# Rows for accumulating DMAs loaded one quarter ahead, their negative right behind the copy of the quarter's opening piece

## The chip, the core and the metric

The kernel runs on one core of one Trainium2 chip. The metric is the device time of one execution in microseconds; the time of the kernel before is the median of three runs. Five engines work beside each other, each in the order of its own instructions: TensorE (PE, with its weight loads as PEld), VectorE (DVE), ScalarE (ACT), GpSimd (POOL) and SyncE (SP). They wait for one another by semaphores. SP, POOL and ACT also issue DMAs.

## The reference

Two layers over 256 tokens of width 2048: each is a norm, a token mixer, a residual add, a norm, a SwiGLU feed-forward block (FFN) and a residual add. Layer 0 has an mLSTM as its mixer, layer 1 an RG-LRU. The change touches only the FFN:

```python
def swiglu(x, w_in, w_out):
    g, u = jnp.split(x @ w_in, 2, axis=-1)
    return (jax.nn.silu(g) * u) @ w_out

...
        h = h + mix
        h = h + swiglu(rms_norm(h, norm_ffn[layer]), ffn_w_in[layer], ffn_w_out[layer])
```

`w_in` is 2048 x 11264 and `w_out` 5632 x 2048, in float32.

## The kernel before

Every float32 product is made of three matmuls. A weight is split into a rounded high part and the low part that is left, an activation likewise, and `product` (L830 to L833) adds high x high (L831), high x low of the weight (L832) and low x high (L833). `split` (L267) makes the two parts of a weight: ACT casts (`L268`), DVE subtracts (`L269`).

The FFN (`ffn`, L810) goes through the 5632 inner columns in eleven **steps** `j` of 512. In a step, `inner` (L835) multiplies the normed input with 512 columns of the gate half and 512 of the up half of `w_in`, in eight pairs `p` of row blocks. Most pairs use seven products of sums of blocks in place of eight; the pairs' weights are `raw`, split into `whix`, `wlox` (of the blocks themselves) and `whit`, `wlot` (of their sums), and the first pair, which is done plainly, into `whi`, `wlo`. At the end of a step PSUM banks `P...` and `Q...` are drained by ACT and DVE into `ds` (L867 to L890), which becomes the step's output `v`; `turn_v` transposes it into `hh`.

The down projection of a step, `hh` with 512 rows of `w_out`, is not done in its own step. `outs` (L906) makes eight **pieces** of it: four quarters `q` of 512 output columns by two blocks `b` of tokens. `between` (L982) runs one piece per pair `p` of the following steps, in the middle of the pair's products. A quarter's opening piece is b = 0, and it loads the quarter. A piece (L951) copies the residual `h` into a PSUM bank (L965, ACT), adds twelve matmuls to it, and copies it back (L976, ACT; these copies are kept in the list `copies`).

The weights of a quarter are four row blocks. Rows 0 and 1 come by SP into `rawo` and are split by ACT and DVE (`whio`, `wloo`). Rows 2 and 3 take work off DVE. POOL loads them into a buffer (named `rawo` in even quarters, `whio` in odd ones, L939), ACT writes the negative of it to `wloo` rounded (L944), POOL issues a second DMA of the same rows that adds them to that negative (L945, the **accumulating DMA**), so that `wloo` holds the low part, and ACT rounds the buffer in place to the high part (L946). The negative is kept behind the copy of the piece before the last one by `after`, which fixes an order between two instructions; otherwise a scheduler orders each engine, and `tc.high_priority(offset=AHEAD)` lets it take an instruction earlier than the place at which it is written.

```python
                            with after(*copies[-2:-1]):
                                nc.scalar.activation(wl, raw, AF.Copy, scale=-1.0)
                            nc.gpsimd.dma_start(wl, src, accum_op=ALU.add)
                            nc.scalar.copy(wh, raw)
```

After step 10 the pieces that are left of step 9 and the eight of step 10 are done in one go, with loads and splits of four row blocks at once (the branch `last` in `load`). In the first step the load of rows 2 and 3 is held back until `v` is there, by a copy of one element on POOL (L938), since the buffers' space is used by something else before.

## Time and profile before

| | |
|---|---|
| median of three runs | 2182.32 us (2180.9 to 2183.56) |
| profiled execution | 2184.34 us |
| its span, first to last instruction | 2182.4 us |
| mean granted TensorE clock | 0.976 |
| DMA | 446.66 MB, mean 205 GB/s |

The span falls into the mLSTM mixer up to about 404 us, the first FFN up to about 1145, the RG-LRU mixer up to about 1440, and the second FFN with the final norm. Times in rows are microseconds from the start of the span. A row of the timeline has start, duration, engine, line, operation, output and inputs; in brackets stands the engine's idle time just before and what ended it. A row of the list of waits has the total, the number and the longest wait. A row that ends in `DMA to landing` has the shortest, median and longest time from the issue of a DMA to its landing. Buffer numbers are left out of the names in the profile: `wloo` is each of the low parts of the down projection.

### The profile page before, as it was taken

How to read it: one execution, taken by the hardware profiler on the slowest of the kernel's cores; microseconds unless marked ns; L12 is line 12 of the kernel's file. 1: busy time of each engine (PE TensorE's matmuls, PEld its weight loads, DVE VectorE, ACT ScalarE, POOL GpSimd, SP SyncE). 2: the span in 40 equal slices, each digit the busy share in tenths (PEclk: the TensorE clock that was granted, in tenths of full speed). 3: DMA queues.
4: the chain of work that ended last, by engine and by line, in shares of the span. 5: the costliest groups of instructions: out<-in, count | busy, mean ns of one | idle time of the engine just before them, and what ended most of it. 6: DMA issues, size and time to landing. Idle time of an engine off the chain costs nothing.

```text
span 2182.4 us, 27890 instructions
## 1 busy us (share of the span) xinstructions
PE 2088.9 (96%) x10430; PEld 1761.3 (81%) x10430; DVE 1736.0 (80%) x1920; ACT 1435.8 (66%) x1755; POOL 205.8 (9%) x222
## 2 busy tenths in 40 slices
PE   9999999998899898989999999999889999898998
PEld 8988888877788787878879999887778778787886
DVE  6655556688799797998976797768879979798896
ACT  5345445556677676867865777655668767686775
POOL 0011110011111110111100000001111111111112
PEclk9999999999999999999999999999999999999999
DMA  7556566566787786886855666656668768688684
GB/s 227 170 163 179 175 194 211 174 204 182 200 256 218 196 247 195 234 243 197 239 175 166 193 189 207 212 174 203 190 202 252 223 193 250 194 236 246 192 237 150
DMA packets 233119, 446.66 MB, mean 205 GB/s; under 512 B 16328, under 2 KB 17048, under 8 KB 232856
## 3 DMA queue, kind: packets, MB, share of 16 engines
q1 hardware_dynamic: 189832, 362.02, 50.1%
q0 software_dynamic: 42432, 81.80, 18.6%
q8 instruction: 81, 1.33, 0.2%
q10 hardware_dynamic: 720, 1.07, 0.1%
q14 instruction: 54, 0.44, 0.1%
HBM read 442.74 MB, written 2.10 MB: 204 GB/s over the span
## 4 chain that ended last, share of the span: by engine, by line
PE 82%; DMA 6%; issue 6%; DVE 2%; ACT 2%; POOL 1%; POOLq 0%; ACTq 0%; SPq 0%; DVEq 0%
PE out L832 7%; PE out L833 7%; PE out L831 6%; PE P L832 6%; PE P L833 6%; PE P L831 5%; DMA wloo<-in_ffn_w_out_dram 5%; PE Q L831 5%; PE Q L832 5%; PE Q L833 5%; PE po L328 3%; PE po L330 3%; PE po L329 3%; PE v L328 1%; PE o L330 1%
## 5 line engine op out<-in xcount | busy, mean ns | idle before, releaser
L244 DVE TENSOR_TENSOR wlo<-raw,whi 128x1024 fp32r<-128x1024 f32 (+1 forms) x226 | 273.6, 1213 | 173.8 <-ACT whi L243 171.4
L268 ACT CAST whit<-sum 128x1024 fp32r<-128x1024 f32 x284 | 296.3, 1052 | 153.9 <-DVE sum L312 147.8
L269 DVE TENSOR_TENSOR wlot<-sum,whit 128x1024 fp32r<-128x1024 f32 x284 | 346.5, 1222 | 54.6 <-ACT whit L268 52.9
L243 ACT CAST whi<-raw 128x1024 fp32r<-128x1024 f32 (+1 forms) x226 | 234.2, 1042 | 194.7 <-PE po L330 40.2
L832 PE MATMUL out<-wloo,hh 128*128 128x512 f32 x704 | 281.6, 400 | 69.1 <-DMA wloo<-in_ffn_w_out_dram 69.0
L269 DVE TENSOR_TENSOR wlox<-raw,whix 128x1536 fp32r<-128x1536 f32 x142 | 249.0, 1754 | 5.1 <-ACT whix L268 4.8
L268 ACT CAST whix<-raw 128x1536 fp32r<-128x1536 f32 x142 | 210.7, 1484 | 37.6 <-PE P L833 32.8
L832 PEld LDWEIGHTS out<-wloo,hh 128*128 128x128 f32 x704 | 134.5, 191 | 102.9 <-DMA wloo<-in_ffn_w_out_dram 73.3
L831 PE MATMUL out<-whio,hh 128*128 128x512 f32 x544 | 212.6, 391 | 1.5 <-ACT whio L268 1.2
L833 PE MATMUL out<-whio,hh 128*128 128x512 f32 x544 | 211.5, 390 | 0.7 <-DVE hh L546 0.7
L976 ACT COPY h<-out 128x512 f32<-128x512 f32 x154 | 89.9, 584 | 169.7 <-PE out L833 169.1
L312 DVE TENSOR_TENSOR sum<-raw 128x1024 f32<-128x1024 f32 x142 | 173.8, 1224 | 3.6
L945 POOL DMA_DIRECT2D wloo<-in_ffn_w_out_dram x78 | 93.3, 1197 | 723.3 <-ACT wloo L944 691.5
L269 DVE TENSOR_TENSOR wloo<-rawo,whio 128x1024 fp32r<-128x1024 f32 (+1 forms) x88 | 118.1, 1342 | 8.6 <-ACT whio L268 8.4
L831 PEld LDWEIGHTS out<-whio,hh 128*128 128x128 f32 x544 | 102.1, 188 | 25.4 <-ACT out L965 2.4
L831 PE MATMUL Q<-whit,p_f 128*128 128x512 f32 x284 | 111.5, 393 | 9.7 <-ACT whit L268 9.7
L833 PEld LDWEIGHTS out<-whio,hh 128*128 128x128 f32 x544 | 102.1, 188 | 22.1 <-DVE hh L546 1.1
L832 PE MATMUL P<-wlox,p_f 128*128 128x512 f32 x284 | 114.6, 403 | 0.0
L268 ACT CAST whio<-rawo 128x1024 fp32r<-128x1024 f32 (+1 forms) x88 | 101.2, 1150 | 18.9 <-PE out L833 16.8
L833 PE MATMUL P<-whix,p_f 128*128 128x512 f32 x284 | 113.2, 398 | 0.0
L831 PE MATMUL P<-whit,p_f 128*128 128x512 f32 x284 | 111.2, 392 | 0.0
L831 PE MATMUL P<-whix,p_f 128*128 128x512 f32 x284 | 111.0, 393 | 0.0
(307 smaller groups left out, 5470.6 us busy)
## 6 DMA issues: line engine op xcount, KB each, us to landing
raw<-in_ffn_w_in_dram SPq DMA_DIRECT2D x352, 512.0 KB, 5.3
rawo<-in_ffn_w_out_dram SPq DMA_DIRECT2D x98, 512.0 KB, 6.2
raw<-in_m_w_in_dram SPq DMA_DIRECT2D x94, 512.0 KB, 3.8
wloo<-in_ffn_w_out_dram POOLq DMA_DIRECT2D x78, 512.0 KB, 7.5
raw<-in_r_w_in_dram SPq DMA_DIRECT2D x64, 512.0 KB, 3.9
rawo<-in_ffn_w_out_dram POOLq DMA_DIRECT2D x40, 512.0 KB, 4.8
whio<-in_ffn_w_out_dram POOLq DMA_DIRECT2D x38, 512.0 KB, 5.3
raw<-in_m_w_out_dram SPq DMA_DIRECT2D x32, 512.0 KB, 3.7
```

The lines of the kernel that those rows point to most:

```text
L243: nc.scalar.copy(hi[:, i:i + step, 0:ncols], r)
L244: nc.vector.tensor_tensor(lo[:, i:i + step, 0:ncols], r, hi[:, i:i + step, 0:ncols].bitcast(F32), op=ALU.subtract)
L268: nc.scalar.copy(hi, src)
L269: nc.vector.tensor_tensor(lo, src, hi.bitcast(F32), op=ALU.subtract)
L312: nc.vector.tensor_tensor(t[:, 0:2, :], raw[:, 1:3, :], raw[:, 3:4, :].broadcast_to([P, 2, NB]), op=ALU.add)
L328: nc.tensor.matmul(o, lhsT=ah[:, bs], rhs=hi, start=(k == 0), stop=False)
L330: nc.tensor.matmul(o, lhsT=al[:, bs], rhs=hi, start=False, stop=(k == nk - 1))
L831: nc.tensor.matmul(o, lhsT=a[0], rhs=b[0], start=start, stop=False, **kw)
L832: nc.tensor.matmul(o, lhsT=a[0], rhs=b[1], start=False, stop=False, **kw)
L833: nc.tensor.matmul(o, lhsT=a[1], rhs=b[0], start=False, stop=stop, **kw)
L945: nc.gpsimd.dma_start(wl, src, accum_op=ALU.add)
L976: copies.append(nc.scalar.copy(hs, o))
```

## The change

Rows 2 and 3 of a quarter are loaded by a function of their own, `load_ahead`, which is run at the second piece (b = 1) of the quarter before; the first of all is run when the first step's pieces are made. The load is ordered behind the last accumulating DMA (`adds`), and the negative behind the newest copy of a piece (`copies[-1:]`, which is that of the opening piece of the running quarter) in place of the one before the newest. The preload of the second piece (`nc.scalar.copy(o, hs)`) is ordered behind the rounding of the buffer. The copy of one element on POOL ahead of the first load from SP is left out. The pieces of a step are made after pair 1 of the next step (after pair 2 in step 1), before it after pair 3; so the quarters' pieces run in pairs 3 to 7 and 0 to 2, and three pieces are left at the end instead of four.

```diff
-        fresh, copies = [True], []
+        fresh, copies, adds, coming = [True], [], [], []
...
-                for i in range(2):
-                    src = wv[:, 2 * i:2 * i + 2, q * NB:(q + 1) * NB]
...
-                    if i == 0:
-                        raw, wh, wl = buffer("raw", F32, ""), buffer("whi", F32R, ""), buffer("wlo", F32R, "")
-                    else:
-
-                        wh, wl = buffer(("raw", "whi")[q % 2], F32R, ""), buffer("wlo", F32R, ("", "1")[q % 2])
-                        raw = wh.bitcast(F32)
+                raw, wh, wl = (buffer(what, dt, 0, q) for what, dt in (("raw", F32), ("whi", F32R), ("wlo", F32R)))
+                nc.sync.dma_start(raw, wv[:, 0:2, q * NB:(q + 1) * NB])
+                with tc.high_priority(offset=AHEAD):
+                    split(wh, wl, raw)
+                for wh, wl in ((wh, wl), ahead.pop(q)):
+                    tiles.extend((wh[:, k, :], wl[:, k, :]) for k in range(2))
...
+            def load_ahead(q):
+
+                wh = buffer(("raw", "whi")[q % 2], F32R, 1, q)
+                wl = buffer("wlo", F32R, 1, q, ("", "1")[q % 2])
+                ahead[q] = wh, wl
+                src = wv[:, 2:4, q * NB:(q + 1) * NB]
+                with tc.high_priority(offset=AHEAD):
                     if j == 0 and q == 0:
 
-                        nc.gpsimd.tensor_copy((wh if i else raw)[0:1, 0, 0:1], v[0][0:1, 0:1])
-                    (nc.gpsimd if i else nc.sync).dma_start(wh if i else raw, src)
-                    with tc.high_priority(offset=AHEAD):
-                        if i:
-
-                            with after(*copies[-2:-1]):
-                                nc.scalar.activation(wl, raw, AF.Copy, scale=-1.0)
-                            nc.gpsimd.dma_start(wl, src, accum_op=ALU.add)
-                            nc.scalar.copy(wh, raw)
-                        else:
-                            split(wh, wl, raw)
-                    tiles.extend((wh[:, k, :], wl[:, k, :]) for k in range(2))
+                        nc.gpsimd.tensor_copy(wh[0:1, 0, 0:1], v[0][0:1, 0:1])
+                    with after(*adds[-1:]):
+                        nc.gpsimd.dma_start(wh, src)
+                    with after(*copies[-1:]):
+                        nc.scalar.activation(wl, wh.bitcast(F32), AF.Copy, scale=-1.0)
+
+                    adds.append(nc.gpsimd.dma_start(wl, src, accum_op=ALU.add))
+                    return nc.scalar.copy(wh, wh.bitcast(F32))
+
+
+            coming.extend(lambda q=q: load_ahead(q) for q in range(4) if j < NJ - 1)
+            if j == 0:
+                coming.pop(0)()
...
                 if not first:
-                    with tc.high_priority(offset=AHEAD):
+
+                    done = [coming.pop(0)()] if b and coming and not last else []
+                    with after(*done), tc.high_priority(offset=AHEAD):
                         nc.scalar.copy(o, hs)
...
-            if left == 0 and p == 3 and late:
+
+            if left == 0 and p == (2 if j == 1 else 1) and late:
```

On POOL the queue of DMAs in two steps in the middle of a layer stood so before (`rawo` and `whio` are the loads, `wloo` the accumulating DMAs):

```order
L939 DMA rawo_4945<-in_ffn_w_out_dram 128x2x512
L939 DMA whio_5081<-in_ffn_w_out_dram 128x2x512
L945 DMA wloo_4946<-in_ffn_w_out_dram 128x2x512
L945 DMA wloo_5082<-in_ffn_w_out_dram 128x2x512
L939 DMA rawo_5199<-in_ffn_w_out_dram 128x2x512
L945 DMA wloo_5200<-in_ffn_w_out_dram 128x2x512
```

And on POOL now, for three quarters in the middle of a layer:

```order
L947 DMA rawo_4838<-in_ffn_w_out_dram 128x2x512
L951 DMA wloo_4839<-in_ffn_w_out_dram 128x2x512
L947 DMA whio_4966<-in_ffn_w_out_dram 128x2x512
L951 DMA wloo_4967<-in_ffn_w_out_dram 128x2x512
L947 DMA rawo_5102<-in_ffn_w_out_dram 128x2x512
L951 DMA wloo_5103<-in_ffn_w_out_dram 128x2x512
```

In every second step the next load stood between a load and its accumulating DMA; now each accumulating DMA stands right behind its own load and ahead of the next.

On ACT, at the end of such a step before (`P_4` is a PSUM bank of the step that ends, `ds` its output, `whi_0` to `whit_1` weights of the next step, `out` the bank of a piece):

```order
L867 COPY ds_5410<-P_4_5504 128x512
L872 COPY ds_5410<-P_4_5504 128x512
L268 CAST whi_0_5914<-raw_0_5911 128x2048
L884 ACTIVATE ds_5410<-ds_5410,rstd_f_3779 128x512
L268 CAST whio_5940<-rawo_5939 128x1024
L944 ACTIVATE wloo_5946<-rawo_5945 128x1024
L976 COPY h<-out_5873 128x512
L946 CAST rawo_5945<-rawo_5945 128x1024
L965 COPY out_5951<-h 128x512
L268 CAST whix_1_5994<-raw_1_5987 128x1536
```

And on ACT now, at the end of the same step:

```order
L867 COPY ds_5436<-P_4_5524 128x512
L872 COPY ds_5436<-P_4_5524 128x512
L268 CAST whi_0_5940<-raw_0_5937 128x2048
L884 ACTIVATE ds_5436<-ds_5436,rstd_f_3779 128x512
L986 COPY h<-out_5899 128x512
L949 ACTIVATE wloo_5967<-whio_5966 128x1024
L268 CAST whix_1_6014<-raw_1_6007 128x1536
L952 CAST whio_5966<-whio_5966 128x1024
L975 COPY out_5965<-h 128x512
```

The negative (L949) has moved behind the copy of the opening piece of quarter 2 (L986), and it is now that of quarter 3; the preload of the second piece (L975) has moved behind the negative, `whix` and the rounding (L952). On TensorE the end of an earlier step reads so now (`out_4965` is the second piece); ahead of these rows stand nine matmuls of pair 7, and ahead of them the opening piece's last:

```order
L831 MATMUL P_3_4944<-whi_0_4940,p_f_3097 128x512
L832 MATMUL P_3_4944<-wlo_0_4941,p_f_3097 128x512
L833 MATMUL P_3_4944<-whi_0_4940,p_f_3097 128x512
L831 MATMUL P_3_4944<-whi_0_4940,p_f_3097 128x512
L832 MATMUL P_3_4944<-wlo_0_4941,p_f_3097 128x512
L833 MATMUL P_3_4944<-whi_0_4940,p_f_3097 128x512
L831 MATMUL P_3_5024<-whix_1_5014,p_f_3118 128x512
L831 MATMUL P_3_4944<-whix_1_5014,p_f_3118 128x512
L831 MATMUL out_4965<-whio_4894,hh_4435 128x512
```

The second piece's first matmul is the eighteenth after the opening piece's last; at the other quarters it is the twenty-fifth.

At the start of a layer's second step ACT had, before:

```order
L545 CAST hh_3995<-tv 128x512 x2
L268 CAST whio_4189<-rawo_4188 128x1024
L944 ACTIVATE wloo_4196<-rawo_4195 128x1024
L946 CAST rawo_4195<-rawo_4195 128x1024
L268 CAST whit_2_4098<-sum_2_4090 128x1024
L268 CAST whi_3_4128<-raw_3_4125 128x2048
L268 CAST whix_4_4163<-raw_4_4156 128x1536
L268 CAST whit_2_4098<-sum_2_4090 128x1024
```

and has now:

```order
L545 CAST hh_3995<-tv 128x512 x2
L949 ACTIVATE wloo_4126<-rawo_4125 128x1024
L952 CAST rawo_4125<-rawo_4125 128x1024
L268 CAST whit_2_4098<-sum_2_4090 128x1024
L268 CAST whi_3_4135<-raw_3_4132 128x2048
L949 ACTIVATE wloo_4217<-whio_4216 128x1024
L268 CAST whit_2_4098<-sum_2_4090 128x1024
L268 CAST whix_4_4190<-raw_4_4183 128x1536
```

A second negative, whose rows POOL loads after the first accumulating DMA, stands ahead of the second half of `whit_2`; before, the load, the negative and the accumulating DMA of that quarter were done ahead of the step.

More of the change, by code (lines that the diff above doesn't have):

```diff
@@ L923, in load @@
                     return
-                for i in range(2):
-                    src = wv[:, 2 * i:2 * i + 2, q * NB:(q + 1) * NB]
-                    def buffer(what, dtype, at):
-                        return pool_of(f"{what}o{at}").tile([P, 2, NB], dtype, tag=f"{what}{i}", name=f"{what}o{j}{q}{i}")
-                    if i == 0:
-                        raw, wh, wl = buffer("raw", F32, ""), buffer("whi", F32R, ""), buffer("wlo", F32R, "")
-                    else:
-                        wh, wl = buffer(("raw", "whi")[q % 2], F32R, ""), buffer("wlo", F32R, ("", "1")[q % 2])
-                        raw = wh.bitcast(F32)
-                    if j == 0 and q == 0:
-                        nc.gpsimd.tensor_copy((wh if i else raw)[0:1, 0, 0:1], v[0][0:1, 0:1])
-                    (nc.gpsimd if i else nc.sync).dma_start(wh if i else raw, src)
-                    with tc.high_priority(offset=AHEAD):
-                        if i:
-                            with after(*copies[-2:-1]):
-                                nc.scalar.activation(wl, raw, AF.Copy, scale=-1.0)
-                            nc.gpsimd.dma_start(wl, src, accum_op=ALU.add)
-                            nc.scalar.copy(wh, raw)
-                        else:
-                            split(wh, wl, raw)
-                    tiles.extend((wh[:, k, :], wl[:, k, :]) for k in range(2))
@@ new lines, in load, with buffer @@
+                raw, wh, wl = (buffer(what, dt, 0, q) for what, dt in (("raw", F32), ("whi", F32R), ("wlo", F32R)))
[4 more added lines that the diff above has]
+                    tiles.extend((wh[:, k, :], wl[:, k, :]) for k in range(2))
+            ahead = {}
+            def buffer(what, dtype, i, q, place=""):
+                return pool_of(f"{what}o{place}").tile([P, 2, NB], dtype, tag=f"{what}{i}", name=f"{what}o{j}{q}{i}")
```

## The prediction

> **What bounds the kernel now.** The page's first part names the engine, the chain of waits says what else stands on the path, and the list of waits says how often.
>
> ```profile
> PE 2088.9 (96%) x10430; PEld 1761.3 (81%) x10430; DVE 1736.0 (80%) x1920; ACT 1435.8 (66%) x1755; POOL 205.8 (9%) x222
> PE 82%; DMA 6%; issue 6%; DVE 2%; ACT 2%; POOL 1%; POOLq 0%; ACTq 0%; SPq 0%; DVEq 0%
> PE out L832 <- DMA wloo<-in_ffn_w_out_dram: 69.0, 10, 7.5
> PE Q L831 <- ACT whit L268: 9.7, 4, 4.6
> ```
>
> TensorE carries the end. It waits for one thing that matters: ten times, 69.0 us together, for the accumulating DMA that makes the low part `wloo` of rows 2 and 3 of a quarter; 9.7 us go to ACT. The chain in order of time has the ten as five in each FFN layer, one for every second step (one pass of the loop over `j`); the second and the last of the first layer:
>
> ```profile
> 571.47 10.65 DMA wloo<-in_ffn_w_out_dram
> ...
> 970.94 10.69 DMA wloo<-in_ffn_w_out_dram
> ```
>
> The timeline around the first shows why it is late.
>
> ```profile
> 570.09 1.08 ACT L944 ACTIVATE wloo<-rawo 128x1024 fp32r<-128x1024 f32 x1
> 570.53 0.72 POOL L939 DMA_DIRECT2D whio<-in_ffn_w_out_dram  x1 [14.46 <-ACT whio L268]
> 571.47 1.22 POOL L945 DMA_DIRECT2D wloo<-in_ffn_w_out_dram  x1 [0.22 <-issue]
> ...
> 582.16 0.80 PE L832 MATMUL out<-wloo,hh 128*128 128x512 f32 x1 [6.92 <-DMA wloo<-in_ffn_w_out_dram]
> ```
>
> ACT makes the negative only at 570.09, behind a crowd of work at the step's end, and POOL issues the accumulate right behind another load: it lands after 10.65 us, against a median of 7.5. PE stands 6.92 us. Afterwards the matmul takes 0.80 us: the clock has dropped too. The windows give the whole price.
>
> ```profile
> 571.47:704.64 133.17, 126.25 (x552) 103.70 (x551) 117.46 (x115) 97.36 (x113) 15.44 (x17) 0.96 0.77 221
> 588.34:708.00 119.66, 119.66 (x536) 98.88 (x535) 112.30 (x109) 94.80 (x110) 15.44 (x16) 1.00 0.77 220
> 583.00:590.00 7.00, 7.00 (x21) 5.45 (x21) 0.50 (x1) 2.69 (x5) 0.83 (x1) 0.62 0.21 80
> 1606.93:1739.54 132.61, 125.67 (x552) 103.32 (x551) 117.47 (x115) 97.37 (x113) 15.46 (x17) 0.97 0.77 222
> ```
>
> The columns are length, then busy time and count for PE, PEld, DVE, ACT, POOL, then the granted clock, DMA share and GB/s. The stretch without a wait does 536 matmuls in 119.66 us, so the 552 of two steps need 123.2. They took 133.17 in the first layer and 132.61 in the second: a late accumulate costs 9.95 or 9.4 us, 6.9 standing and some 3 at a low clock (0.62 in the third row). I take 9.7 for each.
>
> **The change part by part.** *The accumulates.* All ten waits at 9.7 us: **-97 us** if none is left. I test that against the new order. Let S be the start of the last matmul of a quarter's opening piece.
>
> ```profile
> 780.16 0.39 PE L831 MATMUL out<-rawo,hh 128*128 128x512 f32 x1
> 780.61 0.39 PE L833 MATMUL out<-rawo,hh 128*128 128x512 f32 x1
> 781.09 0.59 ACT L976 COPY h<-out 128x512 f32<-128x512 f32 x1 [0.50 <-PE out L833]
> 781.57 1.07 ACT L944 ACTIVATE wloo<-whio 128x1024 fp32r<-128x1024 f32 x1
> 782.53 0.59 ACT L965 COPY out<-h 128x512 f32<-128x512 f32 x1
> 782.94 1.19 POOL L945 DMA_DIRECT2D wloo<-in_ffn_w_out_dram  x1 [7.17 <-ACT wloo L944]
> 783.05 1.06 ACT L946 CAST whio<-whio 128x1024 fp32r<-128x1024 f32 x1
> 783.99 0.73 ACT L887 ACTIVATE ds<-ds,rstd_f 128x512 f32<-128x512 f32 x1
> ```
>
> Two matmuls are 0.45 us, 0.225 each. From S (780.61) the copy to `h` starts at S+0.48, what stands behind it 0.48 later, behind a negative or cast of 1024 columns 0.95, and the accumulate is issued at S+2.3. In the new order PE then has 25 matmuls, the piece b=1 (11 more to its last), 19 matmuls and 7 of the next piece before it reads the new `wloo`: 62 x 0.225 = S+14.0. That leaves 11.7 us to land, 10.7 where a `whit` cast stands ahead of the negative.
>
> ```profile
> DMA to landing us min/median/max: 5.9/7.5/11.3
> DMA to landing us min/median/max: 4.0/5.3/9.0
> ```
>
> The first row is of the tile `wloo`, the second of the loads of `whio` on POOL's queue. The longest accumulate took 11.3, and that beside a load; the new queue puts the next load 6 us behind the accumulate. So the ten go, and what is late next is ACT.
>
> *The load ahead of the negative.* It is issued when the previous quarter's second piece has been multiplied, 30 matmuls (6.75 us) before S, and some 0.6 us later on POOL. With the median of 5.3 us it is there by S-0.9; the negative's slot is S+0.96. Free up to a landing of about 7.1 us, and then ACT, in order, holds back every cast behind it.
>
> *The piece b=1, whose preload now stands behind negative and cast.* In 50 of the steady quarters PE has 25 matmuls (5.6 us) to do first, and ACT needs copy, negative, cast, at most two `whit` and the preload: 0.48+0.48+4x0.95+0.59 = 5.35, plus some 0.15 to restart PE. That just fits; cost 0, and 0.2 where a cast is late. At the step's end (18 times) it doesn't: PE reaches the preloaded piece after 18 matmuls (S+4.05), while ACT has the copy, the negative, `whix` of the next step, the cast, then the preload.
>
> ```profile
> 777.20 1.49 ACT L268 CAST whix<-raw 128x1536 fp32r<-128x1536 f32 x1
> 778.58 2.01 ACT L268 CAST whit<-sum 128x1024 fp32r<-128x1024 f32 x2
> ```
>
> `whix` holds ACT for 1.38, so the preload ends at S+0.48+0.48+0.95+1.38+0.95+0.59 = S+4.83, and PE starts near S+4.95: 0.9 us, **18 x 0.9 = +16**. Bounds: 0, if PE is late for another reason there, to 2 each (a `whix` more), +36.
>
> *The start of each FFN layer* gets worse. Before, one pair of the first loads was done long ahead; now two pairs load, negate and accumulate in turn, and ACT waits for both.
>
> ```profile
> 445.07 0.49 POOL L938 COPY rawo<-ds 1x1 f32<-1x1 f32 x1 [38.06 <-DVE ds L889]
> 445.51 5.24 POOL L938 CAST rawo<-ds 1x1 fp32r<-1x1 f32 x1
> ...
> 455.87 1.06 ACT L944 ACTIVATE wloo<-rawo 128x1024 fp32r<-128x1024 f32 x1 [4.61 <-DMA rawo<-in_ffn_w_out_dram]
> ...
> 459.00 0.79 PE L831 MATMUL Q<-whit,p_f 128*128 128x512 f32 x1 [4.37 <-ACT whit L268]
> ...
> 463.93 1.04 ACT L268 CAST whit<-sum 128x1024 fp32r<-128x1024 f32 x1
> ...
> 465.02 0.50 PE L831 MATMUL Q<-whit,p_f 128*128 128x512 f32 x1 [0.44 <-ACT whit L268]
> ```
>
> The first wait stays, 0.45 us shorter (the small POOL copy ahead of the cast is gone). The second negative then stands ahead of the `whit` that PE took at 465.02. The first accumulate is issued 0.3 us behind its negative, as above, at 456.8 now; the second load follows when that issue (1.2 us) is over, at 458.0. At 7.5 us, the accumulates' median, since the two share the queue, it lands at 465.5; the negative 1.06 and the cast 1.04 end at 467.6, 2.6 after the old 465.0. PE stands some 3.5 us a second time, and I add 1.5 for the clock, half of the 3 above: 2.6 + 1.5 = 4.1 a layer, **+8**. Bounds: a landing of 5.3 and no clock, +1; of 9.0 with 3 us of clock, +14. The Trainium skill ("TensorE: Matmul & The Clock Gate", Part 1) has the clock halve after about one idle window of 3.4 us; by it the second wait lies at the edge, and the clock costs 3 or nothing in each layer instead of my 1.5: an estimate of 3 more or 3 less for the sum. The matmul at 459.00, 0.79 us behind 4.37 us of waiting, agrees; the one at 465.02, behind 0.44, has kept its clock.
>
> *The layer's end.* Three pieces of the last but one step are left over instead of four, and their quarter 3 goes through the accumulate (80 accumulates instead of 78), so DVE loses a split of 2048 columns and ACT gains a copy.
>
> ```profile
> 1099.00:1145.00 46.00, 44.24 (x212) 35.66 (x211) 35.75 (x45) 31.28 (x50) 1.53 (x4) 1.00 0.57 172
> ```
>
> PE idles 1.8 us there, the most to be had. Its first read of the accumulated tile now comes 32 matmuls and eight transposes (taken as half a matmul each) after S, some S+8.1, while issue and median landing give S+9.8: a wait of 1.7. I take +1 a layer, **+2**, bounds -4 and +7.
>
> *DVE.* Two steps need 117.46 us of it in 123.2, 95%. The odd steps show that this works without a wait for TensorE, and the new order takes a `wloo` split out of the step's end. **+4**, bounds 0 and the second rival.
>
> Sum: -97 + 16 + 8 + 2 + 4 = -67. The profiled execution took 2184.3 us (span 2182.4 and 1.9 around it), 2.0 above the median of the three runs, 2182.3: 2117 for an execution like the profiled one, and **2115 us** on the scale of the median.
>
> **The rivals.** *Nothing new waits.* PE, DVE and ACT reach the step's end so that the preload is there, and the second load of a layer lands early: -97 only, 2085 us. For it: TensorE lost 9.7 us to ACT in all before, so ACT keeps up nearly everywhere. Against it: then nothing of 2.9 us stood between copy and preload at the step's end.
>
> *DVE becomes the bound.* In the 133.17 us of two steps it idles 15.7, in the stretch without a wait 7.4. If in-order waits keep its idle time halfway, at 11.6, two steps take 129.1, the ten pairs give 41 instead of 97 less 16, and with +8 and +2 the time is 2151. For it: 95%. Against it: the odd steps, and the work moved out of the step's end.
>
> *The load ahead becomes the wait, and the kernel slower.* ACT stands in every quarter until the load has landed. With d the landing over 7.1 us, the four quarters of a step lose some 4d - 2.4 at PE (three have 1.1 us of room, the step's end 0.9 less than none). The sum without that 16 is -83, 4.6 for each of 18 steps, so it turns slower from d = 1.75, a landing of 8.9 us. At 9.0, the longest of the row above, d is 1.9: 18 x 5.2 = 94, 2182 - 83 + 94 = 2193. For it: some loads do land that late. Against it: the median of 5.3, and the new order, which keeps the accumulate 6 us away. The Trainium skill ("SBUF — State Buffer", the box on the "DVE blocks DMA" trap) lets DVE's two-port operations keep GpSimd from writing descriptors, so that a load from its queue is late; a DVE at 95% would bring this rival nearer. The issues on POOL took 0.72 to 1.22 us with DVE at 88%, which shows no such block.
>
> *The change doesn't do what it says*: the accumulate lands as late for its reader as before. It needs landings over 11.7 us in every second step, and gives 2182. Against it: 11.3 at the most.
>
> **How the numbers follow.** The forecast 0.55, nothing new 0.15, DVE 0.17, slower 0.08, no effect 0.05. The forecast's own range, from the bounds of start, end and step's end that are likely together, is 2098 to 2133. The first three hold 0.87, so the range goes from 2083 to 2153. A measurement of this kernel tells 0.2%, some 4.4 us, from no change: faster 0.87, the same 0.05, slower 0.08.
>
> **What would show it.** Right: no PE wait for `wloo` over 2 us inside the layers; two steps in 124 to 127 us; a PE wait of about 0.9 us before `out` for the preload at each step's end; PE waits for `whit` twice at a layer's start, the second of 3 to 4 us. Wrong: ACT idle before the negatives for the load (third rival), DVE without idle time and PE waiting for `wlot` or `wlox` (second), POOL accumulates that land after 12 us.

## The result and the profile after

| | before | after |
|---|---|---|
| median | 2181.61 us (2180.0 to 2183.56, 4 runs) | 2106.26 us (2103.27 to 2107.66, 4 runs) |
| ratio, 95% interval | 1 | 0.9652 (0.9636 to 0.9669) |
| span of the profiled execution | 2182.4 us | 2105.5 us |
| mean granted TensorE clock | 0.976 | 0.994 |

The kernel is 75 us faster; 67 were forecast. The page of the changed kernel (busy time of the engines, then the chain that ended last, by engine), its list of waits (total, number, longest), and its group row for the matmuls that read `wloo` (busy time and mean ns, then the idle time before them):

```profile
PE 2067.6 (98%) x10430; PEld 1749.1 (83%) x10430; DVE 1729.0 (82%) x1918; ACT 1451.7 (69%) x1763; POOL 198.3 (9%) x224
...
PE 78%; issue 13%; ACT 3%; DVE 2%; DMA 2%; POOL 2%; ACTq 0%; SPq 0%; POOLq 0%; DVEq 0%
```

```profile
PE out L831 <- ACT out L975: 16.3, 20, 2.9
PE Q L831 <- ACT whit L268: 7.6, 2, 4.2
```

```profile
L832 PE MATMUL out<-wloo,hh 128*128 128x512 f32 x704 | 275.6, 392 | 0.0
```

The 69.0 us of waiting for the accumulating DMA are gone without a rest. What TensorE waits for now is ACT: twenty preloads of a piece and two casts of `whit`. Two steps in the windows of the changed kernel, two pairs of the first layer and one of the second:

```profile
565.56:690.32 124.76, 123.51 (x552) 101.76 (x550) 116.97 (x115) 98.48 (x113) 15.53 (x16) 1.00 0.83 236
690.32:814.99 124.67, 123.43 (x552) 101.76 (x550) 116.88 (x115) 98.64 (x113) 15.56 (x16) 1.00 0.84 237
1624.81:1749.53 124.72, 123.48 (x552) 101.69 (x550) 117.03 (x115) 98.65 (x113) 15.59 (x16) 1.00 0.83 236
```

133.17 us have become 124.7, at the full clock, and DVE still idles 7.8 us of them. The end of a step in the timeline, where 18 of the preload waits stand:

```profile
561.70 0.39 PE L833 MATMUL out<-rawo,hh 128*128 128x512 f32 x1
562.18 0.59 ACT L986 COPY h<-out 128x512 f32<-128x512 f32 x1 [1.21 <-PE out L833]
562.66 1.07 ACT L949 ACTIVATE wloo<-whio 128x1024 fp32r<-128x1024 f32 x1
563.63 1.47 ACT L268 CAST whix<-raw 128x1536 fp32r<-128x1536 f32 x1
564.03 1.20 POOL L951 DMA_DIRECT2D wloo<-in_ffn_w_out_dram  x1 [7.70 <-ACT wloo L949]
565.00 1.04 ACT L952 CAST whio<-whio 128x1024 fp32r<-128x1024 f32 x1
565.94 0.59 ACT L975 COPY out<-h 128x512 f32<-128x512 f32 x1
...
566.58 0.50 PE L831 MATMUL out<-whio,hh 128*128 128x512 f32 x1 [0.63 <-ACT out L975]
```

S is 561.70. Copy, negative, `whix`, rounding cast and preload start at S+0.48, 0.96, 1.93, 3.30 and 4.24, the accumulate at S+2.33, each within 0.05 us of the working. PE starts 0.05 us behind the end of the preload, where some 0.12 were taken. The matmul before the wait started at 565.56, so this one comes 1.02 us behind it in place of 0.23: 0.8 lost.

To compare stretches I use one number, **lost time**: over successive matmuls of PE whose starts are more than 0.26 us apart, the sum of what the distance exceeds 0.227 us, the full clock's distance. It holds both the waits and what a slow clock takes behind them. The table takes it from the profiled execution of each kernel. "Start" is 40 us on either side of the first matmul of a layer's down projection, "end" from 35 us ahead of its last to 15 behind, "middle" what lies between; first layer / second layer, in us:

| kernel | median us | start | middle | end |
|---|---|---|---|---|
| before | 2181.61 | 7.5 / 8.0 | 53.2 / 50.8 | 2.2 / 1.5 |
| after | 2106.26 | 7.1 / 6.5 | 12.9 / 13.1 | 4.1 / 3.1 |
| e1 preload first | 2075.95 | 1.0 / 1.1 | 3.6 / 3.3 | 3.1 / 3.0 |
| e2 shift only | 2091.76 | 8.1 / 8.2 | 4.7 / 2.2 | 3.5 / 4.5 |
| e3 POOL order | 2224.0 | 8.0 / 7.9 | 76.1 / 73.9 | 1.9 / 0.8 |
| e4 three casts | 2116.53 | 11.0 / 14.0 | 13.0 / 12.1 | 3.5 / 3.2 |
| e5 start order | 2094.53 | 1.1 / 1.1 | 13.4 / 11.9 | 3.7 / 2.0 |
| e6 no order | 2087.82 | 6.3 / 6.3 | 5.2 / 3.2 | 2.8 / 3.8 |
| e7 late at step end | 2114.64 | 6.0 / 5.3 | 14.0 / 12.5 | 3.9 / 4.8 |
| e8 ahead only | 2122.91 | 5.4 / 5.4 | 19.5 / 19.8 | 5.3 / 5.8 |
| e9 late elsewhere | 2246.13 | 6.5 / 5.3 | 82.0 / 81.0 | 3.2 / 4.4 |

From before to after the middles lose 78 us less, the starts 2 less, the ends 3.5 more: -76.3, and the spans differ by 76.9. So the account closes, and the forecast's term for the start, +8, has the wrong sign. The start of the first layer in the changed kernel:

```profile
443.47 0.51 POOL L945 CAST rawo<-ds 1x1 fp32r<-1x1 f32 x1 [40.54 <-DVE ds L889]
444.29 0.95 POOL L947 DMA_DIRECT2D rawo<-in_ffn_w_out_dram  x1 [0.32 <-POOL rawo L945]
449.56 1.06 ACT L949 ACTIVATE wloo<-rawo 128x1024 fp32r<-128x1024 f32 x1 [0.50 <-DMA rawo<-in_ffn_w_out_dram]
451.71 1.22 POOL L947 DMA_DIRECT2D whio<-in_ffn_w_out_dram  x1
458.63 1.06 ACT L949 ACTIVATE wloo<-whio 128x1024 fp32r<-128x1024 f32 x1 [4.16 <-DMA whio<-in_ffn_w_out_dram]
460.68 0.79 PE L831 MATMUL Q<-whit,p_f 128*128 128x512 f32 x1 [4.16 <-ACT whit L268]
```

The POOL cast, 5.24 us long before, takes 0.51. The first load goes out at 444.29 instead of 451.06, ACT waits 0.50 us for it instead of 4.61, and TensorE's first wait is gone. The one that is left is the second that was forecast: ACT stands 4.16 us at the second negative, whose load landed after 6.9 us where 7.5 were taken, and PE stands 4.16 us for the `whit` behind it. At the end of a layer the new wait is another than forecast, and longer:

```profile
1061.54 1.06 ACT L949 ACTIVATE wloo<-whio 128x1024 fp32r<-128x1024 f32 x1
1062.50 1.89 ACT L268 CAST whio<-rawo 128x2048 fp32r<-128x2048 f32 x1
1064.28 1.04 ACT L952 CAST whio<-whio 128x1024 fp32r<-128x1024 f32 x1
1065.23 0.59 ACT L975 COPY out<-h 128x512 f32<-128x512 f32 x1
1065.87 0.50 PE L831 MATMUL out<-whio,hh 128*128 128x512 f32 x1 [2.87 <-ACT out L975]
```

```profile
1066.89:1070.30 3.41, 3.41 (x9) 2.52 (x8) 3.04 (x4) 2.52 (x2) 0.00 (x0) 0.50 1.06 255
```

It isn't the accumulate that is late here but the preload, behind the negative, a cast of 2048 columns and the rounding cast. The window behind it runs at half the clock. By the starts of the matmuls the wait and this slow stretch lose 4.7 us here, and 4.6 at the end of the second layer.

### The profile page after: what moved, and what is told of

It is laid out like the page before. It is cut to its first block, busy times and chain, and to the rows that moved or that the text cites. A ratio compares the mean times of both kernels' runs of the same rounds, so it can differ in the third digit from the quotient of the medians.

```text
span 2105.5 us, 27920 instructions
## 1 busy us (share of the span) xinstructions
PE 2067.6 (98%) x10430; PEld 1749.1 (83%) x10430; DVE 1729.0 (82%) x1918; ACT 1451.7 (69%) x1763; POOL 198.3 (9%) x224
## 4 chain that ended last, share of the span: by engine, by line
PE 78%; issue 13%; ACT 3%; DVE 2%; DMA 2%; POOL 2%; ACTq 0%; SPq 0%; POOLq 0%; DVEq 0%
PE out L831 6%; PE out L833 6%; PE out L832 6%; PE P L832 5%; PE P L833 5%; PE P L831 5%; PE Q L832 4%; PE Q L831 4%; PE Q L833 4%; PE po L330 3%; PE po L328 3%; PE po L329 3%; PE qk L347 1%; PE qk L345 1%; PE qk L346 1%
## 5 line engine op out<-in xcount | busy, mean ns | idle before, releaser
L832 PE MATMUL out<-wloo,hh 128*128 128x512 f32 x704 | 275.6, 392 | 0.0
L831 PE MATMUL out<-whio,hh 128*128 128x512 f32 x544 | 215.7, 397 | 19.0 <-ACT out L975 16.3
L986 ACT COPY h<-out 128x512 f32<-128x512 f32 x156 | 91.5, 587 | 171.0 <-PE out L833 171.0
L832 PE MATMUL Q<-wlot,p_f 128*128 128x512 f32 x284 | 111.2, 392 | 0.0
L832 PE MATMUL P<-wlot,p_f 128*128 128x512 f32 x284 | 111.1, 391 | 0.0
```

Source lines behind the costliest of these rows:

```text
L831: nc.tensor.matmul(o, lhsT=a[0], rhs=b[0], start=start, stop=False, **kw)
L832: nc.tensor.matmul(o, lhsT=a[0], rhs=b[1], start=False, stop=False, **kw)
L986: copies.append(nc.scalar.copy(hs, o))
```

## The experiments

**e1: the preload first.** The order between the preload of a piece b=1 and the negative is turned round.

```diff
...
-                    with after(*copies[-1:]):
+                    with after(*copies[-1:], *pre):
                         nc.scalar.activation(wl, wh.bitcast(F32), AF.Copy, scale=-1.0)
...
-                    done = [coming.pop(0)()] if b and coming and not last else []
-                    with after(*done), tc.high_priority(offset=AHEAD):
-                        nc.scalar.copy(o, hs)
+                    with tc.high_priority(offset=AHEAD):
+                        pre = nc.scalar.copy(o, hs)
+                    if b and coming and not last:
+                        coming.pop(0)(pre)
```

> The changed kernel with one order turned round: at a piece b=1 the preload is issued first, and the negative and the rounding cast stand behind it. Theory (what is left at a step's end and at a layer's end is the preload behind negative, whix and rounding cast): the 18 waits of some 1.0 us pitch before the piece b=1 at the steps' ends go (18 x 0.75 = 13.5 us), and so does the wait at each layer's end with its half clock (about 3.0 + 1.6 us each, 9 us), so the time is about 2084 us; the accumulate comes one copy (0.5 us) later and still lands in time, since it has 11.7 us of room and lands after 7.9 in the median. Rival (the accumulate has no room to give; what stands in front of the negative makes it late again): PE waits for wloo return in some of the steps, at some 2 us each or more, and the time is 2106 or over. Second rival (DVE at 94% is next): the waits move to wlot or wlox, and the time stays within 2100 to 2106.

Measured: 2075.95 us, 0.9501 of before (0.9486 to 0.9515), 30 us under the changed kernel and the fastest of all. A step's end in its timeline, and a line of its list of waits:

```profile
541.20 0.59 ACT L987 COPY h<-out 128x512 f32<-128x512 f32 x1 [3.06 <-PE out L833]
...
542.63 0.59 ACT L974 COPY out<-h 128x512 f32<-128x512 f32 x1
...
544.10 1.06 ACT L949 ACTIVATE wloo<-rawo 128x1024 fp32r<-128x1024 f32 x1
```

```profile
PE Q L831 <- ACT whit L268: 0.9, 2, 0.4
```

The wait for the preload no longer stands in the list, those for the accumulate don't come back (one of 0.3 us is left), though the negative now starts at S+3.4 (S is 540.72, 0.48 ahead of the copy), and DVE is no obstacle either, with 0.7 us as the longest wait for it in the list: the rivals fall. The gain was larger than expected since the second negative of a layer's start went behind TensorE's `whit` as well: 11.5 us less are lost at the starts. The middles and ends lose 20 less, where 22.5 were expected.

**e2: the shift alone**, in the kernel before.

```diff
-            if left == 0 and p == 3 and late:
+            if left == 0 and p == (2 if j == 1 else 1) and late:
                 work.extend(late.pop()())
```

> The kernel before with one part of the change alone: the pieces of the next list begin at pair 1 (2 for j=1) in place of pair 3. No load a quarter ahead, no negative behind the copy, no rounding cast ahead of a preload. In the order that this gives, the negative stands directly behind the copy to h in three of four quarters and five ACT instructions behind it in the fourth, and POOL issues no load ahead of an accumulate. Theory (the ten waits came of a late negative and of a load queued ahead of the accumulate, in one place of every two steps, whatever causes it): the fourth quarter's accumulate is issued some 3.8 us later than the others, leaving 7.9 us to land against a median of 7.5, so at most short waits remain; the waits of 6.9 us are gone, about -90, and the 18 waits at the steps' ends do not arise: 2085 to 2100 us. Rival (the load ahead and the negative's new place are what removes the waits; the shift of the pieces merely makes room for them): waits for wloo of several us stay in every step or every second one, 2160 to 2182 us.

Measured: 2091.76 us, 0.9573 of before (0.9557 to 0.9589). One line of the diff takes away all ten waits, and is faster than the whole change. The latest negative of a step in its timeline:

```profile
547.71 0.59 ACT L976 COPY h<-out 128x512 f32<-128x512 f32 x1 [3.06 <-PE out L833]
...
551.99 1.06 ACT L944 ACTIVATE wloo<-rawo 128x1024 fp32r<-128x1024 f32 x1
...
553.35 1.20 POOL L945 DMA_DIRECT2D wloo<-in_ffn_w_out_dram  x1 [11.49 <-ACT wloo L944]
```

```profile
PE Q L831 <- ACT whit L268: 10.1, 3, 4.8
```

The accumulate goes out at S+6.1 (S is 547.23) and has 7.9 us until its reader, in place of the 3.8 of before (571.47 to 575.24, where PE began to wait). It landed in 6.3. So the loads a quarter ahead and the negative's new place are not what the ten waits needed. The starts keep their 16 us, with the POOL cast of 5.24.

**e3: the loads on POOL behind the accumulates**, in the kernel before.

```diff
...
-                    (nc.gpsimd if i else nc.sync).dma_start(wh if i else raw, src)
+                    with after(*(adds[-1:] if i else ())):
+                        (nc.gpsimd if i else nc.sync).dma_start(wh if i else raw, src)
...
-                            nc.gpsimd.dma_start(wl, src, accum_op=ALU.add)
+                            adds.append(nc.gpsimd.dma_start(wl, src, accum_op=ALU.add))
```

> The kernel before with the loads on POOL's queue ordered behind the accumulate issued last, and nothing else. In the order that this gives, no load is issued ahead of a waiting accumulate, but the negative now stands eight ACT instructions behind the copy once in every step (some 18 places) where it did so once in two steps (10 places). Theory (the price of a late place is the late negative and the accumulate's own landing of about 7.5 to 7.9 us; the load ahead of it added some 2.8 us): 18 waits of about 4.3 us in place of ten of 7.1, each with up to 2 us at a low clock behind it: 2165 to 2200 us. Rival (the load queued ahead made the wait, the negative's place hardly matters): waits of under 1 us, some 2090 to 2110 us.

Measured: 2224.0 us, 1.0183 of before (1.0166 to 1.02); slower than the theory's 2200. From its list of waits:

```profile
PE out L832 <- DMA wloo<-in_ffn_w_out_dram: 102.1, 18, 6.5
```

18 places instead of ten, as expected, but 5.7 us each instead of 4.3: the accumulates of these places landed in 8.7 to 9.9 us, not 7.9, with the load 0.73 us behind them. Before, with the load ahead of them (by 0.94 us, in each layer's first place by 1.92), they took 9.8 to 11.3. The means are 9.1 and 10.5, so by these two kernels, and if nothing else beside it counts, the load's place is worth about 1.4 us. It isn't what makes the wait, so the rival falls; but the landing isn't a constant, as I had it.

**e4: the POOL cast three times**, in the changed kernel.

```diff
                     if j == 0 and q == 0:
 
+                        nc.gpsimd.tensor_copy(wh[0:1, 0, 1:2], v[0][0:1, 0:1])
+                        nc.gpsimd.tensor_copy(wh[0:1, 0, 2:3], v[0][0:1, 0:1])
                         nc.gpsimd.tensor_copy(wh[0:1, 0, 0:1], v[0][0:1, 0:1])
```

> The changed kernel with the one-element POOL cast at the start of each FFN layer done three times in a row, on three neighbouring elements. In the kernel before the second of two such operations took 5.24 us in both layers and ended as DVE's run of operations with two SBUF inputs ended; in the changed kernel the only one took 0.51. Theory (a POOL operation is held while DVE's run of operations with two SBUF inputs lasts): 0.5, then 5.1 to 5.3 until that run ends (when DVE's L546 starts), then 0.5 us again. First rival (every further operation costs a fixed 5.2 us): 0.5, 5.2, 5.2. Second rival (what took 5.24 was the switch from a copy to a cast): 0.5, 0.5, 0.5. The loads of the layer's start then come some 5.7 us later by the theory; by the working of the prediction, which had kept the 5.24, the start of a layer would then cost some 4 to 5 us more than it does in the changed kernel: about 2115 us; by the second rival 2107.

Measured: 2116.53 us, 0.9691 of before (0.9674 to 0.9708). POOL and DVE in its timeline, and its wait for `whit`:

```profile
443.88 0.68 DVE L315 TENSOR_TENSOR sum<-sum,raw 128x512 f32<-128x512 f32 x1
444.10 0.51 POOL L945 CAST rawo<-ds 1x1 fp32r<-1x1 f32 x1 [40.46 <-DVE ds L889]
...
444.55 5.25 POOL L946 CAST rawo<-ds 1x1 fp32r<-1x1 f32 x1
...
447.42 2.35 DVE L269 TENSOR_TENSOR wlot<-sum,whit 128x1024 fp32r<-128x1024 f32 x2
...
449.69 1.28 DVE L546 TENSOR_TENSOR hh<-tv,hh 128x512 fp32r<-128x512 f32 x2
...
449.75 0.17 POOL L947 CAST rawo<-ds 1x1 fp32r<-1x1 f32 x1
```

```profile
PE Q L831 <- ACT whit L268: 14.5, 4, 4.6
```

0.51, 5.25, 0.17 us (0.51, 5.25, 0.17 in the second layer): neither a fixed price of a further operation nor the switch from copy to cast. The second ends at 449.80, as DVE goes over from subtractions with two SBUF inputs to L546, which reads PSUM. The Trainium skill ("SBUF — State Buffer", Who interferes with whom) says that a VectorE instruction with two SBUF inputs contends with a GpSimd instruction that reads SBUF, and that the later one blocks. The rows agree: the first cast started beside one such DVE instruction (L315) and ended 0.05 us behind it, and the second was held through five in a row. That DVE is the cause rests on the times and this rule; the DVE run itself was not taken away. For the account it matters more that with the 5.25 us back, `whit` is waited for four times, as the prediction had worked out, and the starts lose 25.0 us against 15.5 before: +9.5 where +8 was forecast.

**e5: the order turned round at the layers' starts only**, in the changed kernel.

```diff
+                    opens = j == 0 and q == 0
-                    done = [coming.pop(0)()] if b and coming and not last else []
+                    done = [coming.pop(0)()] if b and coming and not last and not opens else []
                     with after(*done), tc.high_priority(offset=AHEAD):
-                        nc.scalar.copy(o, hs)
+                        pre = nc.scalar.copy(o, hs)
+                    if b and opens:
+                        coming.pop(0)(pre)
```

The negative takes `*pre` as in e1.

> The changed kernel with the order turned round at one place of each layer only: the second negative of an FFN layer (first step, first quarter's piece b=1) stands behind that piece's preload, and so behind the whit that PE stands for. All later quarters are as in the changed kernel. Theory (the first wait of a layer start is gone through the shorter POOL cast, and what is left of it is ACT standing at the second negative for its load, some 4 us, with half a clock behind it): the excess at each layer start falls from 7.1 and 6.5 us to about 1, so 2106 - 11.5 = about 2095 us. Rival (what the first experiment gained beyond the 18 step ends came from the layer ends or from DVE, and the start is bound by the load itself): 2104 to 2107 us, with the wait for whit replaced by one for wloo.

Measured: 2094.53 us, 0.9596 of before (0.9581 to 0.9611), 11.7 under the changed kernel. From its waits:

```profile
PE out L831 <- ACT out L976: 16.9, 20, 2.9
...
PE Q L831 <- ACT whit L268: 0.9, 2, 0.4
```

The starts' waits go and nothing over 0.4 us takes their place; the twenty preloads stay as they were.

**e6: the preload not ordered behind the rounding cast**, in the changed kernel.

```diff
-                    with after(*done), tc.high_priority(offset=AHEAD):
+                    with tc.high_priority(offset=AHEAD):
                         nc.scalar.copy(o, hs)
```

> The changed kernel with one part undone: the preload of a piece b=1 is no longer ordered behind the rounding cast of the quarter's load. In the order that this gives, the negative stands directly behind the copy to h in three of four quarters and four ACT instructions behind it at the step's end; the starts of the layers are unchanged. Theory (the 18 waits at the steps' ends and the ones at the layers' ends are the preload behind that cast, and an accumulate issued some 3 us later there still has about 8.8 us to land, against 7.9): the waits for out of the preload's line go, 2106 - 13.5 - 6 = 2085 to 2092 us, the layer starts' 7 us stay. Rival (without that order the negative is late again as in the kernel before): waits for wloo at the steps' ends, 18 times some 2 us or more with a slower clock behind, 2106 to 2150 us.

Measured: 2087.82 us, 0.9564 of before (0.9548 to 0.958), 18.4 under the changed kernel. The first two lines of its waits:

```profile
PE Q L831 <- ACT whit L268: 6.6, 2, 3.3
PE tv L898 <- DVE ds L889: 4.7, 4, 2.0
```

No wait for the preload and none for `wloo`: the one `after` cost 18 us and bought nothing. At the layers' ends waits for `ds` (4.7 us in four) stand in the preload's place. e5 and e6 together make 30.2 us, e1 gained 30.3.

**e7: a late negative at the step's end**, in the changed kernel: the negative, accumulate and rounding cast of q=3 are written behind the copy of the piece b=1.

```diff
...
+                if q == 3 and j:
+                    held_back.append(rest)
+                    return None
+                return rest()
...
-                    done = [coming.pop(0)()] if b and coming and not last else []
+                    done = [d for d in ([coming.pop(0)()] if b and coming and not last else []) if d is not None]
...
                         copies.append(nc.scalar.copy(hs, o))
+                if b and held_back:
+                    held_back.pop()()
```

Here `rest` holds the last lines of `load_ahead`, from the negative on. The line with `done` undoes one thing more: the preload at the step's end no longer stands behind the rounding cast.

> The changed kernel with the negative of one quarter a step (q=3, j=1 to 9, 18 places) put behind the copy to h of the piece b=1 in place of that of the opening piece. Nothing else stands near: its load has long landed, and the next load on POOL's queue comes later. Theory (lateness alone makes the wait, through a landing of 7.9 us in the median whatever stands beside it): the negative comes 8.1 us later, the accumulate is issued at about S+10.4 for a reader at S+14.0, so PE stands 7.9 - 3.6 = 4.3 us at wloo in each of the 18 places, and the slow clock behind each adds some 2.6 as in the kernel before: 2106 + 18 x 6.9 = about 2230 us, range 2205 to 2240. Rival (the load queued ahead of it made the accumulate of the kernel before late; with none beside it, it lands in some 5 us): waits of 1 to 2 us, no slow clock, 2125 to 2145 us.

Measured: 2114.64 us, 0.9692 of before (0.9674 to 0.971): 8 us slower than the changed kernel where 120 were expected, and below the rival's range too. Its list of waits:

```profile
PE out L832 <- DMA wloo<-in_ffn_w_out_dram: 9.6, 5, 4.1
```

Three of the five waits stand at the ends of steps, at most 1.6 us long; the two others are at the layers' ends. The 8 us are not the price of the lateness alone: TensorE's waits for the preload fell from 16.3 us in 20 places to 4.6 in 11, as the order behind the rounding cast is gone at the step's end. Taken without that gain of 11.7 us, the late negatives cost some 20.

My count was off in two ways. q=3 is the quarter at the step's end, and its reader stands 65 matmuls and eight transposes behind S (15.9 us), not 62 matmuls; and the accumulate issued at 571.47 landed in 5.9 us, just in time, though it went out later behind S (9.9 us) than that of before (8.7). The DMA view of the kernel before between 571.00 and 582.20, and of this one between 571 and 577.5, shows what was issued while one such accumulate was under way (count, size, median time to landing):

```profile
raw<-in_ffn_w_in_dram SPq DMA_DIRECT2D x4, 512.0 KB, 6.8
whio<-in_ffn_w_out_dram POOLq DMA_DIRECT2D x1, 512.0 KB, 5.4
wloo<-in_ffn_w_out_dram POOLq DMA_DIRECT2D x1, 512.0 KB, 10.7
rawo<-in_ffn_w_out_dram SPq DMA_DIRECT2D x1, 512.0 KB, 9.4
```

```profile
wloo<-in_ffn_w_out_dram POOLq DMA_DIRECT2D x1, 512.0 KB, 5.9
rawo<-in_ffn_w_out_dram POOLq DMA_DIRECT2D x1, 512.0 KB, 7.5
rawo<-in_ffn_w_out_dram SPq DMA_DIRECT2D x1, 512.0 KB, 6.1
```

Six other transfers of 512 KB stand in the first, over 11.2 us, two in the second, over 6.5 us, to which two loads of `raw` have to be added: they were issued at 568.56 and 568.98 and landed by 573.54. POOL's next load, which I had expected later, went out 0.73 us behind the accumulate, at 572.21. For every accumulate I added up what part of each other DMA's time, from issue to landing, fell into its own. In the changed kernel the 80 landings follow 5.0 us plus 1.2 for each such transfer (correlation 0.80); in the kernel before 5.7 plus 1.0 (0.86). This is a relation in the traces and a weak one: no experiment added or took away transfers alone, and a longer landing also meets more of them. With the mean number of other transfers under way, which a longer landing doesn't raise by itself, the correlation is 0.60 in the changed kernel, 0.70 in the kernel before and only 0.22 in e7.

**e9: the same at another quarter**, `q == 2` in place of `q == 3` in the diff of e7.

> The seventh experiment once more, at another quarter: the negative of q=2 (18 places) in place of that of q=3 is put behind the copy to h of the piece b=1. In the seventh, the late quarter turned out to be the one at the step's end, whose reader stands seven matmuls further back than I had counted (S + 69 matmuls, not 62), and its accumulate landed in 5.9 us, with fewer other transfers beside it than in the kernel before, where it took 10.6. Here the reader stands 26 matmuls (5.9 us) behind the last of the piece b=1, and PE's order is that of the changed kernel, so the accumulate, issued 2.3 us behind that matmul, has 3.5 us. Theory (the lateness makes a wait of the landing less the room, and the landing is about 5.0 us and 1.2 more for each other transfer of 512 KB beside it, as the 80 accumulates of the changed kernel have it): no landing is under 5.9, so PE stands at least 2.4 us in each of the 18 places, and 4.7 where two or three transfers run beside it: 2106 + 18 x 2.4 = 2149 with short waits and no slow clock, up to 2106 + 18 x (4.7 + 2.6) = 2237 with long ones; most likely about 2190. Rival (a late negative costs next to nothing as long as no load stands at the accumulate, as the seventh experiment could be read): 2106 to 2120 us.

Measured: 2246.13 us, 1.0299 of before (1.0281 to 1.0316), slower than the kernel before; above the expected range by 9 us.

```profile
PE out L832 <- DMA wloo<-in_ffn_w_out_dram: 95.9, 18, 6.0
```

18 waits of 5.3 us: the late negative brings the waits back where the reader leaves some 4 us (in the first place PE begins to wait at 561.14, 4.0 behind the issue; the expectation had 3.5). The landings took 9.3 us in the mean. The shortest landing of any run here is 5.9, so 1.9 of the 5.3 follow from the lateness alone; the rest is the long landing. The late accumulate at 557.12, with one load of `raw`, one of `rawo` and one of POOL's beside it for most of its time and two more of `raw` for a part, landed in 9.6 us; over all 80 of this kernel the relation is again 5.0 plus 1.2 each (0.90). Each place costs 140/18 = 7.8 us, 5.3 of standing and 2.5 of slow clock. The rival's condition isn't met, since in all 18 places POOL's next load went out 0.73 us behind the accumulate; but it did so in 16 places of e7 as well, where the accumulates landed in 5.9 to 7.6 us, and with landings of 5.9 throughout, 18 waits of 1.9 would still give 2140 us, above the rival's range. So it falls.

**e8: the change without the shift.** The list of a step is made early, its pieces start where they did before.

```diff
             if left == 0 and p == (2 if j == 1 else 1) and late:
-                work.extend(late.pop()())
+                staged.append(late.pop()())
+            if left == 0 and p == 3 and staged:
+                work.extend(staged.pop())
```

> The changed kernel without the shift: the load a quarter ahead, the negative behind the copy of the opening piece, the orders, all as changed, but the pieces of the next list begin at pair 3 as in the kernel before (the list itself is made at pair 1 or 2, so that its loads can go ahead). In the order that this gives the negative stands directly behind the copy in most quarters and one ACT instruction behind it in three of twelve. It is the counterpart of the second experiment, which had the shift alone. Theory (the second experiment took the waits away because the late place was gone, not because of the shift as such; any way of having the negative early and POOL's loads out of its way does it): no PE wait for wloo over 2 us, and waits for the preload behind the rounding cast at some of the steps' ends: 2090 to 2115 us. Rival (the shift is the part that removes the waits, and the load ahead does nothing for them): waits for wloo as in the kernel before, 2160 to 2190 us.

Measured: 2122.91 us, 0.9728 of before (0.9707 to 0.9749); 8 above the range of the theory. From its waits:

```profile
PE out L831 <- ACT out L975: 14.5, 14, 3.9
...
PE P L831 <- ACT whix L268: 6.2, 6, 1.3
```

No wait for an accumulate: this half of the change, too, takes all ten away by itself. Its middles lose 13 us more than those of the changed kernel, not at preloads (14.5 us in 14 waits against 16.3 in 20) but at `whix`, at low parts that DVE makes, and in many gaps that are too short for the list.

## Why the prediction was right

**The accumulates, -97: right.** The windows give (133.17 - 124.76) + 2 x 0.8 = 10.0 us for each late place of the first layer and (132.61 - 124.72) + 1.6 = 9.5 in the second: 97.5 for ten. The cause was told in part only: "behind a crowd of work at the step's end, and POOL issues the accumulate right behind another load". The late negative is what brings the waits: e9 brings them back by it, and e2 and e8, where it comes earlier, have none; the load ahead of the accumulate is worth some 1.4 us of the landing (e3). How much a late one costs hangs on the reader's distance: before, PE began to wait 3.8 us behind the issue, so that even the shortest landing on record, 5.9, would have made a wait of 2.1 of the 6.9. The rest is the landing of 10.6 us, and why it is so long is open: longer landings have more transfers beside them in the traces (e7 against e9), but no run shows that these make them longer. Either half of the change was enough (e2, e8), which the prediction, taking the change as one, did not see; a list of what each half moves would have shown it.

**The step's end, +16: right.** 18 times 0.8 us, 14 in all, through the chain that was worked out; e6 and e1 take it away. The 0.1 us that is missing in each place is the time that PE takes to start again, 0.05 in the row where 0.12 had been taken, without a row for it.

**The layers' starts, +8: wrong, -2 measured.** The step that failed is "The first wait stays, 0.45 us shorter". I took the cast's 5.24 us as its own duration and kept it when the copy ahead of it went; it was the time for which POOL was held, and the operation that comes first took 0.5. With the hold put back (e4), the rest of the term holds: +9.5.

**The layers' ends, +2: too small.** The preload's wait there and the slow clock behind it lose 4.7 and 4.6 us, about 9 in place of 2. The table fits: the middles fell by 78, of which the accumulates and the step's ends explain 97.5 - 14 = 83.5; the 5.5 that are missing, and a part of the 3.5 of the "end" column, are this term. The step was "a wait of 1.7" for the accumulated tile. That wait didn't come; the preload stood behind the negative and a cast of 2048 columns, 2.87 us, with a stretch of half clock. The rule found for the step's end, applied here with the wider cast, would have given it.

**DVE, +4: nothing seen.** It idles 7.8 us of 124.76, and no wait of TensorE for it inside the FFN stands in the list, so that rival falls. The errors are about -10 (start), -4 (DVE), -2 (step's end), +7 (layer's end): -9 together, against the -8 by which the median came out lower. That the sum is so near is in part luck: -16 and +7 stand against each other.

**The other rivals.** "Nothing new waits", at 2085 us, is not what the change gives: TensorE waits for twenty preloads and twice for `whit`. Only without them (e1) does the time come below it. The loads ahead were in time:

```profile
DMA to landing us min/median/max: 4.1/5.3/8.1
```

These are POOL's loads of `whio` after the change, none at the 8.9 from which that rival decided; those of `rawo` took 5.8 at most. ACT stood for such a load 9.7 us in all, 8.1 of them at the layers' starts. The accumulates landed within 10.2 us, short of the 11.7 that the last rival needed.

**What each part is worth.** The shift gives 91 us alone, the rest of the change 59 alone, both 75: together they save the same wait only once, and the order of the preload behind the cast (18 us) and of the second negative ahead of TensorE's `whit` (12 us) are paid on top. Without these two, 107 (e1).

## What to carry to other kernels

When a wait ends at a DMA, work out three times before choosing a cure: when it can be issued, when its reader comes, and what else is being transferred then; a one-line shift of the consumers was worth more here than loading earlier. Every instruction that is put "right behind" another one pushes what stood there: list what it pushes, at the odd places (start, end) too, where the casts are wider and the loads not yet there. A tiny operation with a long duration may be held by something: ask what runs beside it before keeping its duration in a sum.

## What was not expected of the hardware

An operation of one element on POOL took 0.51, 5.25 or 0.17 us by its place (e4). The first started beside one DVE operation with two SBUF inputs and ended 0.05 us behind that one; the second was held for the five that followed; the third came behind them. Why the first got through between two of DVE's operations and the second didn't is open. DMA issues on POOL, in contrast, took 0.7 to 1.3 us with DVE at 94%.

The clock fell to 0.50 for 3.41 us behind a single wait of 2.87 us (row of 1066.89), and for twice that, 6.83, behind the 4.16 at the layer's start. The Trainium skill ("TensorE: Matmul & The Clock Gate", Part 1) gives a window of about 3.4 us that runs freely; the 3.41 us agree, and a wait below it can be enough here. In the prediction I had taken a wait near 3.4 as the edge. The traces give no such edge: a wait of 2.02 us in e6 (to 1062.37, with one of 0.36 ahead of it) was followed by 3.41 us at 0.50, while in e5 the wait of 2.87 us at the end of the second layer (to 2051.24) was followed by none.

An accumulating DMA of 512 KB landed in 5.9 us at best and in 11.3 at worst, with the same issue and the same size; the longer landings have more other transfers beside them, which isn't shown to be the cause.
